# A cast load issued ahead of building the identity, in a sparse 3x3 convolution

## The chip, the cores and the metric

The kernel runs on one core of one Trainium2 chip. The metric is device time in microseconds; the median of the runs counts. The profile is of one execution, and its span runs from the first to the last instruction of the program.

## The reference

The reference is a 3x3 convolution with padding 1 over a batch of 16 images, 64 channels in, 128 channels out, 64x64 pixels, in float32. Nine tenths of the weights are zero, and the reference skips those; the result is that of a dense convolution.

```python
batch, c_in, h, w, c_out, k = 16, 64, 64, 64, 128, 3
...
for kh in range(k):
    for kw in range(k):
        if weight[co, ci, kh, kw] != 0:
            output[b, co] += weight[co, ci, kh, kw] * x_pad[b, ci, kh:kh+h, kw:kw+w]
```

## The kernel before

Images are taken in eight pairs. A pair fills the 128 partitions: 64 channels of one image, 64 of the other. Each pair is worked in four blocks of 16 rows. TensorE multiplies each image's half with the weights of one tap (64 x 128) and adds up the taps in PSUM (`product`, L120 to L141).

There are two kinds of block. A direct block (`direct`, L143) sums all nine taps, 8 rows at a time; ScalarE and VectorE copy the sums to the output tile `o`. Only the first block of the first pair is direct. All the others are of the kind `twos` (L150): GpSimd adds two neighbouring rows to `s` (L153), TensorE multiplies `s` with the middle row of taps once for both, ScalarE copies this shared part to `pc` (L160), TensorE makes the rest for even and for odd rows, and VectorE adds the two parts into `o` (L167). So a direct block doesn't need GpSimd, and all later blocks do. It also needs only the rows at the top of the image.

The order on every engine is the order of the program text (`manual_schedule`): nothing is moved by a scheduler, and each engine works through its own list, waiting where it must.

The opening is laid out as follows. SyncE issues two plain loads: the weights (`w_sb`, L60), and the first 18 rows of pair 0 as float32 (`x_head`, L62). GpSimd builds a 128x128 identity in bf16 (`make_identity`, L64: one MEMSET and one select by index, in masks.py). After it, still on GpSimd, comes the load of the first pair's other 46 rows (L65), which casts float32 to bf16 on its way into `xs[0]`, and then seven cast loads of whole pairs (L67). SyncE's loads go through the hardware queue q1, GpSimd's cast loads through the software queue q0; in each queue the transfers stand in the order of their issue.

Meanwhile TensorE runs 27 multiplications of zeros (L74). When the weights have landed, VectorE and ScalarE cast them to bf16 (L91), TensorE transposes them by multiplying with the identity (L97, the first reader of `ident`), and the results are copied to `wT` (L110 to L114, differences at L101). When `x_head` has landed, VectorE casts its first nine rows and ScalarE the other nine (L87), into the upper rows of `xs[0]`. The direct block (TensorE, L134) reads these. The first `s` reads rows 16 to 31, so it needs the load of L65.

A pair's two output tiles are stored by SyncE, 2 MB each (L187); for the last pair in halves of 1 MB (L184). Seven output tiles take turns. At the end SyncE waits for the stores (L213, launch code).

Of the kernel before, what the change touches and what calls it, by code (L numbers as in the profile page):

```python
# [27 lines left out]
def kernel(  # L28
# [6 lines left out]
    nc = tc.nc  # L35

    B, C_IN, H, W = x.shape
# [3 lines left out]
    HEAD = 18  # L41
# [13 lines left out]
    def pair(p):  # L55
        return x[2 * p : 2 * p + 2].rearrange("n i h w -> (n i) h w")

    xs = [x_pool.tile([128, H, W], BF16, name=f"x{p}") for p in range(NP)]
    w_sb = const_pool.tile([C_OUT, C_IN * KH * KW], FP32, name="w_sb")
    nc.sync.dma_start(out=w_sb, in_=weight.rearrange("o i kh kw -> o (i kh kw)"))  # L60
    x_head = const_pool.tile([128, HEAD, W], FP32, name="x_head")
    nc.sync.dma_start(out=x_head, in_=pair(0)[:, 0:HEAD, :])  # L62
    ident = const_pool.tile([128, 128], BF16, name="ident")
    make_identity(nc, ident)  # L64
    nc.gpsimd.dma_start(out=xs[0][:, HEAD:H, :], in_=pair(0)[:, HEAD:H, :])  # L65
    for p in range(1, NP):
        nc.gpsimd.dma_start(out=xs[p], in_=pair(p))  # L67

# [149 lines left out]
```

## Time and profile before

| what | value |
|---|---|
| median of 6 runs | 127.69 us |
| lowest and highest run | 127.37 and 128.45 us |
| the profiled execution's own time | 127.9 us |
| its span | 126.1 us |
| mean granted TensorE clock | 0.957 |
| busy: PE, DVE, ACT, POOL | 110.5, 82.3, 38.1, 40.7 us |
| DMA packets, bytes, mean rate | 4044, 42.70 MB, 339 GB/s |
| HBM read and written | 17.07 and 33.55 MB |

PE is TensorE, PEld its weight loads, DVE is VectorE, ACT is ScalarE, POOL is GpSimd, SP is SyncE. Starts are microseconds from the span's beginning. The DMA row of the page gives, for each fortieth of the span, the mean busy share of the core's 16 DMA engines, in tenths. A cast load counts with the bytes that it writes, which are half of those it reads. A DMA's time to landing runs from the start of the issuing instruction to the last update of its semaphore. In the waits, a row names who waited, for whom, the total in microseconds, how often, and the longest.

### The profile page before, as it was taken

How to read it: one execution, taken by the hardware profiler on the slowest of the kernel's cores; microseconds unless marked ns; L12 is line 12 of the kernel's file. 1: busy time of each engine (PE TensorE's matmuls, PEld its weight loads, DVE VectorE, ACT ScalarE, POOL GpSimd, SP SyncE). 2: the span in 40 equal slices, each digit the busy share in tenths (PEclk: the TensorE clock that was granted, in tenths of full speed). 3: DMA queues.
4: the chain of work that ended last, by engine and by line, in shares of the span. 5: the costliest groups of instructions: out<-in, count | busy, mean ns of one | idle time of the engine just before them, and what ended most of it. 6: DMA issues, size and time to landing. Idle time of an engine off the chain costs nothing.

```text
span 126.1 us, 2486 instructions
## 1 busy us (share of the span) xinstructions
PE 110.5 (88%) x1002; PEld 56.0 (44%) x1002; DVE 82.3 (65%) x135; ACT 38.1 (30%) x70; POOL 40.7 (32%) x45
## 2 busy tenths in 40 slices
PE   6689999999999999999999999999999999980000
PEld 6433454545454545444554555455545554430000
DVE  0352277777777777777787778777877787773000
ACT  4521533333333333332433333333333333330000
POOL 7807443333333333333333333333333330000000
PEclk9999999999999999999999999999999999997555
DMA  4999999999999999999999999999999999999990
GB/s 128 222 217 208 216 221 223 213 166 333 333 294 340 338 312 317 307 333 307 431 447 416 421 416 436 447 431 408 421 431 452 416 426 426 421 418 418 421 385 29
DMA packets 4044, 42.70 MB, mean 339 GB/s; under 512 B 448, under 2 KB 448, under 8 KB 832
## 3 DMA queue, kind: packets, MB, share of 16 engines
q1 hardware_dynamic: 2880, 34.44, 65.5%
q0 software_dynamic: 1152, 8.09, 31.6%
q8 instruction: 8, 0.13, 0.4%
q14 instruction: 4, 0.03, 0.1%
HBM read 17.07 MB, written 33.55 MB: 401 GB/s over the span
## 4 chain that ended last, share of the span: by engine, by line
PE 83%; DMA 4%; DVE 1%; issue 1%; DVEq 0%; SPq 0%
PE ps L134 83%; DMA x_head<-in_x_dram 4%; DVE o L167 1%; DVEq L213 0%; DVE x L87 0%; SPq L60 0%; DVEq L167 0%
## 5 line engine op out<-in xcount | busy, mean ns | idle before, releaser
L134 PE MATMUL ps<-x,wT 64*128 64x504 bf16 (+3 forms) x780 | 91.5, 382 | 1.5 <-DVE x L87 1.5
L167 DVE TENSOR_TENSOR o<-ps,pc 128x512 f32<-128x512 f32 x124 | 77.8, 686 | 22.1 <-PE ps L134 19.8
L134 PEld LDWEIGHTS <-wT 64*128 64x128 bf16 x966 | 52.5, 96 | 55.0 <-issue 4.9
L153 POOL TENSOR_TENSOR s<-x 128x512 bf16<-128x512 bf16 x31 | 35.6, 1152 | 60.8 <-PE ps L134 42.9
L160 ACT COPY pc<-ps 128x512 f32<-128x512 f32 x62 | 33.3, 589 | 64.0 <-issue 61.8
L134 PE MATMUL ps<-s,wT 64*128 64x512 bf16 (+1 forms) x186 | 25.5, 377 | 0.0
L148 DVE COPY o<-ps 128x512 f32<-128x512 f32 x2 | 1.4, 692 | 4.9 <-PE ps L134 4.9
L74 PE MATMUL ps<-idle_rhs 128*128 128x128 bf16 x27 | 3.1, 313 | 1.0 <-DVE idle_rhs L71 1.0
L67 POOL DMA_DIRECT2D x<-in_x_dram x7 | 3.7, 567 | 0.0
L74 PEld LDWEIGHTS <-idle_rhs 128*128 128x128 bf16 x27 | 2.8, 148 | 1.0 <-DVE idle_rhs L71 1.0
L147 ACT COPY o<-ps 128x512 f32<-128x512 f32 x2 | 1.2, 586 | 6.2 <-PE ps L134 6.2
L91 DVE CAST w_bf<-w_sb 128x192 bf16<-128x192 f32 (+1 forms) x4 | 1.2, 383 | 2.7 <-DMA w_sb<-in_weight_dram 2.7
L91 ACT ACT_TABLE_LOAD x1 | 1.3, 1283 | 0.7 <-PEq L202 0.7
L87 DVE CAST x<-x_head 128x576 bf16<-128x576 f32 x1 | 0.5, 460 | 1.6 <-DMA x_head<-in_x_dram 1.6
L97 PE MATMUL ps<-ident,w_bf 128*128 128x128 bf16 x9 | 1.2, 304 | 0.2 <-DVE w_bf L91 0.2
L91 ACT CAST w_bf<-w_sb 128x64 bf16<-128x64 f32 (+1 forms) x2 | 0.7, 416 | 1.6 <-DMA w_sb<-in_weight_dram 1.6
L97 PEld LDWEIGHTS <-w_bf 128*128 128x128 bf16 x9 | 0.7, 122 | 0.7 <-DVE w_bf L91 0.6
L101 DVE TENSOR_TENSOR wT<-ps,wT 128x384 bf16<-128x384 f32 x2 | 1.0, 548 | 0.0
L87 ACT CAST x<-x_head 128x576 bf16<-128x576 f32 x1 | 0.7, 672 | 0.4 <-DMA x_head<-in_x_dram 0.4
L65 POOL DMA_DIRECT2D x<-in_x_dram x1 | 0.7, 702 | 0.1
L71 DVE MEMSET idle_rhs<- 128x64 uint32 x1 | 0.1, 112 | 0.8 <-PEq L202 0.8
L110 ACT CAST wT<-ps 128x384 bf16<-128x384 f32 x1 | 0.5, 478 | 0.4 <-PE ps L97 0.4
(8 smaller groups left out, 1.9 us busy)
## 6 DMA issues: line engine op xcount, KB each, us to landing
out_dram<-o SPq DMA_DIRECT2D x14, 2048.0 KB, 18.1
x<-in_x_dram POOLq DMA_DIRECT2D x7, 1024.0 KB, 29.6
out_dram<-o SPq DMA_DIRECT2D x4, 1024.0 KB, 10.4
x<-in_x_dram POOLq DMA_DIRECT2D x1, 736.0 KB, 8.6
x_head<-in_x_dram SPq DMA_DIRECT2D x1, 576.0 KB, 5.2
w_sb<-in_weight_dram SPq DMA_DIRECT2D x1, 288.0 KB, 2.9
```

Source lines behind the costliest of these rows:

```text
L67: nc.gpsimd.dma_start(out=xs[p], in_=pair(p))
L74: nc.tensor.matmul(idle_ps, idle_rhs, idle_rhs, start=True, stop=True)
L87: copy(out=xs[0][:, a:b, :], in_=x_head[:, a:b, :])
L91: copy(out=w_bf4[:, g, a:b, :], in_=w_v[:, k : k + b - a, :])
L97: nc.tensor.matmul(wps[:, j, :], src, ident, start=True, stop=True)
L101: nc.vector.tensor_tensor(out=wT[:, g], in0=wps, in1=wT[:, G1], op=SUB)
L134: nc.tensor.matmul(ps[n][:, lo:hi, c_lo:c_hi], tap(g, kw, n), src[q, a:b:step, c_lo + kw - 1 : c_hi + kw - 1], start=(i == 0), stop=(i == ...
L147: nc.scalar.copy(out=o[0][:, r0 : r0 + rows, :], in_=ps[0])
L148: nc.vector.tensor_copy(out=o[1][:, r0 : r0 + rows, :], in_=ps[1])
L153: nc.gpsimd.tensor_tensor(out=s, in0=xs[p][:, r0 : r0 + 16 : 2, :], in1=xs[p][:, r0 + 1 : r0 + 16 : 2, :], op=ADD)
L160: nc.scalar.copy(out=c, in_=shared[n])
L167: nc.vector.tensor_tensor(out=o[n][:, first : r0 + 16 : 2, :], in0=ps[n], in1=pc[n], op=ADD)
```

## The change

The GpSimd load of rows 18 to 63 of pair 0 is issued ahead of the identity's two instructions instead of after them. Everything else, and the order on every other engine, stays as it was.

```diff
@@ -60,9 +60,9 @@
     nc.sync.dma_start(out=w_sb, in_=weight.rearrange("o i kh kw -> o (i kh kw)"))
     x_head = const_pool.tile([128, HEAD, W], FP32, name="x_head")
     nc.sync.dma_start(out=x_head, in_=pair(0)[:, 0:HEAD, :])
+    nc.gpsimd.dma_start(out=xs[0][:, HEAD:H, :], in_=pair(0)[:, HEAD:H, :])
     ident = const_pool.tile([128, 128], BF16, name="ident")
     make_identity(nc, ident)
-    nc.gpsimd.dma_start(out=xs[0][:, HEAD:H, :], in_=pair(0)[:, HEAD:H, :])
     for p in range(1, NP):
         nc.gpsimd.dma_start(out=xs[p], in_=pair(p))
```

## The prediction

> **What bounds the kernel now.** I read the page from its end: first the DMA part, then the chain, then the waits of SyncE's queue, then GpSimd's own timeline, and last the DMA view cut into short stretches of the opening. The span in 40 slices, and the queues, come first:
>
> ```profile
> span 126.1 us, 2486 instructions
> ...
> PE   6689999999999999999999999999999999980000
> ...
> DMA  4999999999999999999999999999999999999990
> ...
> q1 hardware_dynamic: 2880, 34.44, 65.5%
> q0 software_dynamic: 1152, 8.09, 31.6%
> ```
>
> PE is full from the third slice on, but it stops 12 us before the end, while the DMA row is full from the second slice to the last but one. The queues' packets took 65.5 + 31.6 + 0.4 + 0.1 = 97.6% of what 16 engines have, 123.1 us of 126.1. The first packet starts at 1.77 us, so some 123 us of transfers lie between 1.77 us and the end. The chain "that ended last" follows compute instructions, and ends with VectorE:
>
> ```profile
> 113.87 0.60 DVE o L167
> ```
>
> That is 114.47 us; 11.6 us of span come after it. SyncE's waits say what for:
>
> ```profile
> SPq L187 <- DVE o L167: 94.9, 14, 22.6
> SPq L184 <- DVE o L167: 10.5, 4, 5.3
> SPq L213 <- DMA out_dram<-o: 9.2, 4, 2.4
> ```
>
> The last row is the closing wait for the stores. The issues and their times to landing show the backlog behind it:
>
> ```profile
> out_dram<-o SPq DMA_DIRECT2D x14, 2048.0 KB, 18.1
> x<-in_x_dram POOLq DMA_DIRECT2D x7, 1024.0 KB, 29.6
> out_dram<-o SPq DMA_DIRECT2D x4, 1024.0 KB, 10.4
> x<-in_x_dram POOLq DMA_DIRECT2D x1, 736.0 KB, 8.6
> x_head<-in_x_dram SPq DMA_DIRECT2D x1, 576.0 KB, 5.2
> ```
>
> A 2 MB store alone is 2.097 MB / 0.425 TB/s (the mean of 62 to 114 us) = 4.9 us, but its median is 18.1 us, and the shortest of all 18 stores took 8.6 us. Each store found at least 8.6 - 4.9 - 1.0 (issue to first packet, as for w_sb: 0.74 to 1.77) = 2.7 us of other transfers ahead of it. So I take the kernel to be bound by its DMA engines, with PE 3 to 4 us ahead of them. The chain's 83% PE names the longest compute chain, not the end.
>
> The opening, as GpSimd lived it (start, length, instruction):
>
> ```profile
> 0.73 0.20 POOL masks.py:197 MEMSET ident<- 128x128 bf16 x1 [0.29 <-POOLq L202]
> 1.01 0.29 POOL masks.py:199 TENSOR_SCALAR_AFFINE_SELECT ident<-ident 128x128 bf16<-128x128 bf16 x1
> 1.43 0.70 POOL L65 DMA_DIRECT2D x<-in_x_dram  x1
> 2.12 3.71 POOL L67 DMA_DIRECT2D x<-in_x_dram  x7
> 10.20 3.35 POOL L153 TENSOR_TENSOR s<-x 128x512 bf16<-128x512 bf16 x3 [4.37 <-DMA x<-in_x_dram]
> ```
>
> The load that moves is issued at 1.43 and lands 8.6 us later, about 10.0. GpSimd then waits for it and makes s at 10.20; PE takes up s only at 13.64 us, after the direct block. And the DMA view of 3.60 to 4.38 us, whole, has one queue alone in it:
>
> ```profile
> DMA packets 38, 0.17 MB, mean 219 GB/s; under 512 B 1, under 2 KB 1, under 8 KB 38
> ## 3 DMA queue, kind: packets, MB, share of 16 engines
> q1 hardware_dynamic: 38, 0.17, 95.7%
> ```
>
> No packet of GpSimd's queue (q0) moves before 4.39 us, 2.96 us after its issue. Engines had gone straight from weights to x_head (the first x_head packets start at 2.70, the last engine's at 3.28), and in the packet records an engine that finishes x_head goes on to q0 some 6 ns later, never before. Only the first to finish stood idle, from 4.27 to 4.39.
>
> **What the Trainium skill says.** "DMA: Bandwidth & Descriptors", section "Issuing engines are not separate DMA queues": transfers issued by SyncE and GpSimd run on the same 16 engines, and a second issuer saves issue time only. The trace agrees: every engine is taken from 1.77 us on, by q1 and then q0. Its section "Queues, rings and completion order" says an engine alternates between queues at packet boundaries, a packet being several descriptors. Here no x_head piece was split by q0, as if all that one engine carries of x_head were one such packet; that fits, though one trace can't prove it. Its section "Latency and other measured facts" gives about 1 us to the first byte on GpSimd's path; this trace has 2.96 us from issue, or 2.26 us from the end of the 0.70 us instruction, and I use those.
>
> **The change part by part.** Nothing is added or removed: the same ten GpSimd instructions, in another order.
>
> The load of rows 18 to 63 moves past the MEMSET (0.20), the select (0.29) and the gaps between them: 1.43 - 0.73 = 0.70 us earlier, so issued at 0.73. It moves past no DMA on its own queue; on SyncE's side it is now issued beside w_sb (0.74) and before x_head (1.16), where it used to come after both. With the same 2.96 us its first packet could start at 3.69 instead of 4.39. All engines have begun x_head by 3.28, so it still queues behind x_head on each. Direct gain: the one idle spell, 4.39 - 4.27 = 0.12 us of one engine in 16, or 0.01 us of DMA time.
>
> The identity moves 0.70 us later: MEMSET at 1.43, select done at about 1.30 + 0.70 = 2.00. Its reader, the first transpose (L97), starts at 4.22 after w_bf, cast from weights that land at 3.64. It is hidden by 2.2 us of waiting for weights; without that cover it would cost 0.70 us of PE's start, which itself has 3 to 4 us of stores to hide behind.
>
> The seven loads at L67 start where they did, 2.12, as the sum of the work ahead of them is unchanged: 0.
>
> If the load does land up to 0.7 us sooner, the first s is made sooner; PE wants it at 13.64, and it was there at 11.35: 0.
>
> What is not visible in the trace of before is how the engines behave when q0 becomes ready earlier. There is a slow stretch: 354 GB/s at 2.8 to 3.6 us, 219 at 3.60 to 4.38, though only x_head moves. From 4.38 to 6.2, x_head's 0.15 MB and q0's 0.18 MB written (0.36 read, for q0 casts 4 bytes to 2) are 0.51 MB in 1.82 us, 280 GB/s, against about 2 x 210 = 420 at 10 to 15 us. Lost: 0.78 x (1 - 219/420) + 1.82 x (1 - 280/420) = 0.37 + 0.61 = about 1.0 us. Its cause I can't read: it starts while GpSimd issues (until 5.83) and before q0 moves. Upper end of a gain: all of it goes, -1.0. Upper end of a loss: it starts 0.7 us earlier and ends when it did, 0.7 x 0.48 = +0.3, or it covers everything from 2.0 us, 1.6 x 0.48 = +0.8. I take 0, as the seven issues that fill 2.12 to 5.83 stay put.
>
> The sum: 126.1 - 0.01 + 0 + 0 = 126.1 of span, with 1.8 us around it 127.9 as profiled. The median of the runs, 127.69, is 0.2 below that execution; on it the likeliest is 127.6 to 127.7. Half a per cent, 0.64 us, is about what this kernel's measurement tells from no change; the six runs alone spread over 1.1 us.
>
> **Rivals.** *Gain (chance 0.22).* An earlier ready q0 lets engines flow from x_head into it without the slow stretch. In its favour: in the packet records the two engines that reached q0 first, at 4.39 and 4.47, needed 2.3 and 2.1 us for a first piece that takes 0.46 later, as if it weren't quite ready. Against: the end is set by the slowest engine, and the slowest at the end (124.51 us; the next was done near 123.7) shows its delay after 62 us, not here. Worth -0.7 to -1.0, from 127.69: 126.9.
>
> *Slower (0.16).* The slow stretch is what an engine does with both queues alive, and now begins 0.7 us or more earlier, during weights and x_head. The stretch began 0.8 us before q0's first packet. It decides if that packet comes at 3.0 us or sooner, 2.3 us after the new issue or less: then weights and x_head run at about 219 GB/s from 2.2 us on, 1.4 x 0.48 = +0.7, up to the +0.8 above: 128.5. x_head itself would land later than 6.38 and PE start later than 6.92, but that costs nothing until PE's 3 to 4 us are used up.
>
> *The compute chain decides (0.03, inside the last).* If q0 got ahead of x_head's packet on an engine, x_head would wait for 8 x 0.455 = 3.6 us there, and PE start at 10.5; with the last stores then needing 4.9 + 1.5 us after PE's end, about 124.9 to 125.5 against 125.0 now: no more than +0.5.
>
> *It doesn't do what it says.* In the built program the load does stand ahead of MEMSET and select, so this is no rival for the order; it is one for the time, since the transfer is hidden anyway. That is my forecast.
>
> **How the numbers follow.** No change 0.62, at 127.6, own range 127.1 to 128.2; gain 0.22 at 126.9; slower 0.16 at 128.5. The range takes in the gain's middle and most of the loss: 126.9 to 128.5. A few of the gain case's outcomes stay inside half a per cent, and a few of the first case's drift out with the spread of runs; the chances stay 0.22, 0.62, 0.16.
>
> **What would show it.** Right: L65 starts near 0.73 and the select ends near 2.0; L67 from 2.1; transposes still from about 4.2; the first q0 packet near 3.7 to 4.3, with x_head landing within 0.3 us of 6.38; the DMA row full from the second slice on; the last compute near 114.5 and the span within 0.6 us of 126.1. Wrong: x_head landing near or after 7 us, with a low GB/s from 2 us on (the slower rival), or over 350 GB/s, reads counted, right through 3.6 to 5.8 us and a span near 125.3 (the gain). The forecast also fails if the DMA row shows holes after 62 us, since then PE's start would count after all.

## The result, and the profile after

The changed kernel took 127.56 us in the median of 35 runs, and the kernel before 127.79 in 72 runs beside it: ratio 0.9979, 95% interval 0.9964 to 0.9994. The medians are over all runs; the ratio leaves out those in a slower state, four of the 35. By the ratio it is 0.27 us less: a gain clear of the noise, but less than half of the half per cent below which the prediction spoke of no change. The forecast was 127.6. The lowest runs are nearly alike (127.23 and 127.31): what the change did is bring more runs near them. 28 of the 72 runs before lay under 127.65 us, and 22 of the 35 after.

The profiled execution has these lines in the page's head and slices:

```profile
span 125.6 us, 2486 instructions
...
PE   6588999999999999999999999999999999910000
...
DMA  4999999999999999999999999999999999999980
```

The picture is that of before: DMA engines taken from the second slice to the end, PE done some 15 us ahead of it (13 before). The chain of work ends with

```profile
111.17 0.60 DVE o L167
```

which is 2.7 us sooner than before, while the span is only 0.5 us shorter. In SyncE's waits that time comes back as a longer closing wait for the stores (9.2 before, 12.1 now):

```profile
SPq L187 <- DVE o L167: 91.9, 14, 19.9
SPq L213 <- DMA out_dram<-o: 12.1, 4, 4.9
```

and in the issues, with KB and median time to landing, into longer queues for the stores (18.1 and 10.4 before):

```profile
out_dram<-o SPq DMA_DIRECT2D x14, 2048.0 KB, 20.1
x<-in_x_dram POOLq DMA_DIRECT2D x7, 1024.0 KB, 31.3
out_dram<-o SPq DMA_DIRECT2D x4, 1024.0 KB, 12.5
x<-in_x_dram POOLq DMA_DIRECT2D x1, 736.0 KB, 8.4
x_head<-in_x_dram SPq DMA_DIRECT2D x1, 576.0 KB, 4.9
```

GpSimd's opening, by its timeline:

```profile
1.23 0.70 POOL L63 DMA_DIRECT2D x<-in_x_dram  x1 [0.79 <-POOLq L202]
1.92 0.23 POOL masks.py:197 MEMSET ident<- 128x128 bf16 x1
2.22 0.29 POOL masks.py:199 TENSOR_SCALAR_AFFINE_SELECT ident<-ident 128x128 bf16<-128x128 bf16 x1
2.46 3.73 POOL L67 DMA_DIRECT2D x<-in_x_dram  x7
9.75 3.36 POOL L153 TENSOR_TENSOR s<-x 128x512 bf16<-128x512 bf16 x3 [3.55 <-DMA x<-in_x_dram]
```

The load starts at 1.23, only 0.20 us sooner than before, and not at 0.73, where the MEMSET used to start. As GpSimd's first instruction here, the DMA issue began 0.50 us later than the MEMSET had; in the kernel before, MEMSET and select filled that time. The other loads start 0.34 us later than before. The moved load's first packet starts at 4.54 us, 3.31 us after the issue, and so later than before (4.39, 2.96 us after). Yet it lands at 1.23 + 8.4 = 9.6 instead of 10.0, and x_head at 6.1 instead of 6.4. The stretch of 3.60 to 4.38 us has the same queue alone, at the same pace:

```profile
DMA packets 38, 0.18 MB, mean 224 GB/s; under 512 B 0, under 2 KB 0, under 8 KB 38
```

The difference comes after it. In the DMA view of 4 to 7 us, the kernel before:

```profile
DMA packets 127, 0.59 MB, mean 197 GB/s; under 512 B 16, under 2 KB 16, under 8 KB 127
## 3 DMA queue, kind: packets, MB, share of 16 engines
q0 software_dynamic: 61, 0.36, 67.2%
q1 hardware_dynamic: 66, 0.23, 37.1%
```

and the changed one:

```profile
DMA packets 142, 0.68 MB, mean 226 GB/s; under 512 B 16, under 2 KB 16, under 8 KB 142
## 3 DMA queue, kind: packets, MB, share of 16 engines
q0 software_dynamic: 76, 0.45, 74.6%
q1 hardware_dynamic: 66, 0.23, 30.0%
```

As many packets of x_head, but 15 more of the moved load. That is one place where the two executions differ; the experiments ask whether the gain comes from there, and whether TensorE, 2.7 us sooner, has a part in it.

### The profile page after: what moved, and what is told of

It is laid out like the page before. It is cut to its first block, busy times and chain, and to the rows that moved or that the text cites. A ratio compares the mean times of both kernels' runs of the same rounds, so it can differ in the third digit from the quotient of the medians.

```text
span 125.6 us, 2486 instructions
## 1 busy us (share of the span) xinstructions
PE 107.4 (86%) x1002; PEld 58.5 (47%) x1002; DVE 82.3 (66%) x135; ACT 38.1 (30%) x70; POOL 40.7 (32%) x45
## 4 chain that ended last, share of the span: by engine, by line
PE 78%; DMA 7%; issue 1%; DVE 1%; POOL 1%; DVEq 0%; POOLq 0%
PE ps L134 78%; DMA x<-in_x_dram 7%; DVE o L167 1%; POOL s L153 1%; DVEq L213 0%; POOLq L153 0%; POOLq L202 0%; DVEq L167 0%; POOLq masks.py:199 0%
## 5 line engine op out<-in xcount | busy, mean ns | idle before, releaser
L134 PE MATMUL ps<-x,wT 64*128 64x504 bf16 (+3 forms) x780 | 88.8, 373 | 1.5 <-DVE x L87 1.5
L134 PEld LDWEIGHTS <-wT 64*128 64x128 bf16 x966 | 55.1, 94 | 49.9 <-issue 1.9
```

Of the source, the lines that this page charges most:

```text
L134: nc.tensor.matmul(ps[n][:, lo:hi, c_lo:c_hi], tap(g, kw, n), src[q, a:b:step, c_lo + kw - 1 : c_hi + kw - 1], start=(i == 0), stop=(i == ...
```

## The experiments

Every kernel was timed beside the kernel before, and the ratios are to that. Three theories stood: **opening** (the engines move more in the first 8 us, and the end follows), **gap** (the half microsecond that the identity now puts between the first cast load and the others is what helps), and **pace** (TensorE's direct block took 6.9 us in the profile before and 4.0 in that after; runs with the slow pace are the long ones, and the change only makes them rarer).

**The two kernels once more**, unchanged.

> The changed kernel once more, as it is, beside the others on the same chip. If the small gain is there: ratio 0.9965 to 0.9995. A second profile tells what repeats: x_head landing near 6.1 and the moved load near 9.6 (they were 6.4 and 10.0 before), its issue near 1.23, the later loads from 2.46; and whether TensorE's direct block takes 4.0 us again as in the first profile after, or 6.9 as before. If the direct block's pace is a matter of chance, it differs without the end differing.

> The kernel before once more, as it is, for a second profile of the opening. If the first profile was typical: x_head lands near 6.4, the moved load near 10.0, and the span is 0.4 us longer than the changed kernel's. If the first was one of the long runs by chance (its 127.9 us are above the median): x_head near 6.1, the load near 9.7, span near 125.7. Ratio 1.000 within 0.0015.

Measured: 0.9979 (0.9963 to 0.9995) for the changed kernel, 0.9989 (0.9970 to 1.0008) for that of before. So the gain repeats. The second profiles are less plain. In that of the changed kernel x_head landed at 6.6 and the moved load at 10.1, later than expected (6.1 and 9.6). In that of before they landed at 6.4 and 10.4, as a typical one should, but its span was not 0.4 us longer than the changed kernel's: it was 125.5 us against 125.6. A span of one execution doesn't show the gain, then; why, comes out below. And the second profile of before has TensorE's direct block at the fast pace, with no change made:

```profile
6.95 3.98 PE L134 MATMUL ps<-x,wT 64*128 64x512 bf16 x36 [1.50 <-DVE x L87]
```

The pace is a matter of chance in the kernel before, so TensorE's 2.7 us between the first two profiles need not be the change's doing. In the traces' clock records the full clock is first recorded at 12.9 us in the first profile of before, at 5.3 in the second and at 4.6 in the first of the changed kernel, which fits the three paces. "TensorE: Matmul & The Clock Gate" of the Trainium skill, section "Part 1: The HAM clock gate", describes a free-running window of activity that decides when the matrix clock comes up; chance of this kind fits that (4.0 to 6.9 us were seen for this block), though no run here shows the window.

**Is it TensorE's pace?** Two kernels: that of before with 60 instead of 27 multiplications of zeros (the full clock is recorded from 6.5 us on, ahead of the block), and the changed one with 4.

```diff
-    for _ in range(27):
+    for _ in range(60):
```

and

```diff
-    for _ in range(27):
+    for _ in range(4):
```

> The kernel before, with nothing but 60 instead of 27 multiplications of zeros, so that TensorE's clock is up before the direct block whenever x_head lands. Theory 'pace of the direct block': the long runs of the kernel before are those in which the direct block runs slowly (6.9 us instead of 4.0), so that the stores come 2 us later and the engines run short of them late in the run; the change makes such runs rarer, and does nothing else. Then this kernel has no long runs either: ratio to before 0.996 to 0.998, at or under the changed kernel's 0.9979, lowest runs as before, few above 127.65 us. Theory 'opening': the gain comes from the transfers of the first 10 us alone; then the multiplications change nothing: 0.999 to 1.001, long runs as often as before.

> The changed kernel with 4 instead of 27 multiplications of zeros, so that TensorE has done little when the direct block starts and that block should run slowly (6 to 7 us) in every run. Theory 'pace of the direct block': the gain is gone, ratio to before 1.000 to 1.004, most runs above 127.65 us. Theory 'opening': ratio 0.997 to 0.999 like the changed kernel.

Measured: before with 60 0.9994 (0.9977 to 1.0011), its block at 3.98 us; changed with 4 0.9983 (0.9966 to 1.0000), its block at 6.53 us. Timed side by side, the two have medians of 127.71 and 127.43 us, and 9 and 16 of 22 runs under 127.65. The theory of pace had the opposite order. The gain stays with the load's place, and the theory of pace falls, though the two ratios' intervals overlap.

**Is it the gap?** The kernel before with two MEMSETs between the load and its followers; and the changed kernel with the identity behind all loads, so without the gap.

```diff
     nc.gpsimd.dma_start(out=xs[0][:, HEAD:H, :], in_=pair(0)[:, HEAD:H, :])
+    pad = const_pool.tile([128, 128], BF16, name="pad")
+    for _ in range(2):
+        nc.gpsimd.memset(pad, 0.0)
     for p in range(1, NP):
```

and

```diff
     nc.gpsimd.dma_start(out=xs[0][:, HEAD:H, :], in_=pair(0)[:, HEAD:H, :])
-    ident = const_pool.tile([128, 128], BF16, name="ident")
-    make_identity(nc, ident)
     for p in range(1, NP):
         nc.gpsimd.dma_start(out=xs[p], in_=pair(p))
+    ident = const_pool.tile([128, 128], BF16, name="ident")
+    make_identity(nc, ident)
```

> The kernel before with two MEMSETs of 128x128 on GpSimd between the first cast load (L65, where it was, at 1.43) and the seven later loads, which so start at about 2.65 instead of 2.12. The change did two things to the queue: it issued the first load 0.20 us earlier and opened a gap of 0.5 us after it. If the gap alone brings the gain: ratio 0.997 to 0.999. If the earlier issue brings it: 0.999 to 1.001.

> The changed kernel with the identity built after all eight cast loads, so that the first load keeps its new place (1.23) and the later ones follow at once (1.93 instead of 2.46), without a gap. The identity is ready only near 6.2, the transposes move from 4.3 to 6.3 and TensorE's first block to about 8.5. If the earlier issue brings the gain: ratio 0.996 to 0.999, in spite of TensorE's 1.5 to 2 us of delay. If the gap brings it: 0.999 to 1.001. If TensorE's chain decides: 1.008 or more.

Measured: gap alone 1.0000 (0.9984 to 1.0016); identity last 1.0001 (0.9983 to 1.0018). The gap alone brings nothing. The second kernel is not as clean as was hoped: its opening is that of the changed kernel (load landed at 9.3), but the gain is not in its time. TensorE stood idle for 2.4 us before the transposes, waiting for the identity, and its last store was issued at 114.5. But the changed kernel with 4 multiplications had its last store as late (114.6) and kept its gain. By its time alone the identity-last kernel came out as the theory of the gap had it. The times so leave open that the gain needs both, the earlier load and the gap after it; the records below speak against that, for one execution.

**A later queue.** Ten MEMSETs ahead of the first cast load of the kernel before.

```diff
     make_identity(nc, ident)
+    pad = const_pool.tile([128, 128], BF16, name="pad")
+    for _ in range(10):
+        nc.gpsimd.memset(pad, 0.0)
     nc.gpsimd.dma_start(out=xs[0][:, HEAD:H, :], in_=pair(0)[:, HEAD:H, :])
```

> The kernel before, with ten more MEMSETs of a 128x128 tile on GpSimd ahead of the first cast load, so that all of GpSimd's loads are issued about 2.0 us later (L65 near 3.4, first packet of its queue near 6.4). DMA-opening theory (time is set by how fully the 16 engines work in the first 7 us, and the slow stretch of x_head belongs to GpSimd's queue coming alive): x_head runs at 350 to 400 GB/s throughout and lands near 4.8 to 5.2, then engines stand idle until about 6.4, some 1.5 us each; set against the 1.0 us of slow stretch that is gone, the end is 0.3 to 0.8 us later, ratio 1.002 to 1.006. Rival, slow stretch belongs to x_head itself: x_head still lands at 6.1 to 6.4, engines idle 0.5 to 1 us in the mean and the later load adds that: 1.004 to 1.010. Rival, compute chain decides: PE starts when x_head lands, the first s comes 2 us later, near 12.2, still before PE wants it if PE runs at the pace of before: 1.000.

Measured: 1.0084 (1.0055 to 1.0113), the load issued at 3.75 (3.4 was expected), its first packet at 5.15 (6.4 was expected), x_head landed at 5.2. The DMA view of 2.80 to 4.30 us shows x_head without the slow stretch,

```profile
DMA packets 173, 0.62 MB, mean 413 GB/s; under 512 B 22, under 2 KB 22, under 8 KB 173
```

where the changed kernel has

```profile
DMA packets 115, 0.44 MB, mean 293 GB/s; under 512 B 11, under 2 KB 11, under 8 KB 115
```

and then, from 4.3 to 5.2 us, little moved at all:

```profile
DMA packets 27, 0.09 MB, mean 97 GB/s; under 512 B 10, under 2 KB 10, under 8 KB 27
```

So the slow stretch goes with GpSimd's first cast load, and x_head alone doesn't have it. But to be rid of it in this way is dear: the engines waited for the queue, and nearly all then needed 0.7 to 1.6 us for the first piece of the cast load, which takes 0.46 later. The end is 1.1 us later than before, for 2.3 us of delay in the issue. The expected 1.002 to 1.006 was too low, as it did not count those slow first pieces.

**The followers later.** Fifteen MEMSETs between identity and the seven loads of the changed kernel.

```diff
     make_identity(nc, ident)
+    pad = const_pool.tile([128, 128], BF16, name="pad")
+    for _ in range(15):
+        nc.gpsimd.memset(pad, 0.0)
     for p in range(1, NP):
```

> The changed kernel, with fifteen more MEMSETs on GpSimd between the identity and the seven later loads, so that those are issued about 3 us later (from 5.5 instead of 2.46), while the load that was moved keeps its place. If the slow stretch (x_head at about 220 GB/s from 3.6 us) comes from the issuing of the seven loads: x_head lands near 4.9 to 5.2 instead of 6.1, the tail of pair 0 near 8.6, and the end is 0.7 to 1.0 us earlier, ratio to before 0.990 to 0.994. If it comes from the first cast load coming alive, or from x_head itself: x_head lands at 6.1 as in the changed kernel, the later loads are still queued in time (the tail lands at 9.6), ratio 0.997 to 0.999 as for the changed kernel.

Measured: 1.0033 (1.0012 to 1.0054), slower than the changed kernel beside it (0.9979), and outside both of the ranges expected; x_head at 6.0 and the first load at 9.5, as in that one. The slow stretch is not due to the issuing of the seven loads. A part of the loss is at the next joint, where the engines go on from the first cast load to the second. From 8.0 to 10.5 us this kernel has

```profile
DMA packets 81, 0.49 MB, mean 197 GB/s; under 512 B 16, under 2 KB 16, under 8 KB 33
```

against, in the changed kernel with 60 multiplications,

```profile
DMA packets 92, 0.58 MB, mean 231 GB/s; under 512 B 16, under 2 KB 16, under 8 KB 36
```

The followers are issued from 6.58, and engines begin to be through with the first load at 8.3: twelve of the first pieces of pair 1 took 0.7 to 1.3 us instead of 0.62. So slow first pieces were seen at both joints at which engines reached a cast load soon after its issue. They don't account for the whole loss: by 20 us this kernel had read 6.98 MB, and the changed kernels of the table below 7.06 in the mean. At 0.42 MB per us that is an estimated 0.2 us, of 0.7 us lost in time.

**The records of the kernels side by side.** By the traces' records of single packets: of the 128 pieces (packets) of the first cast load, how many took over 0.65 us, and the longest; what the loads and stores had moved by 8.0 and by 62 us (a cast piece counts twice its written bytes); when the load landed; the span of that execution.

| kernel | load issued | long pieces, longest | MB by 8 us | MB by 62 us | landed | span | ratio |
|---|---|---|---|---|---|---|---|
| before | 1.43 | 2, 2.31 us | 1.82 | 24.56 | 10.0 | 126.1 | |
| before again | 1.43 | 6, 2.30 | 1.85 | 24.81 | 10.4 | 125.5 | 0.9989 |
| before, gap | 1.43 | 11, 2.33 | 1.79 | 24.63 | 10.2 | 125.8 | 1.0000 |
| before, 60 | 1.42 | 7, 2.65 | 1.82 | 24.72 | 10.4 | 125.6 | 0.9994 |
| before, late queue | 3.75 | 21, 1.55 | 1.53 | 24.18 | 10.8 | 127.1 | 1.0084 |
| changed | 1.23 | 1, 1.05 | 2.00 | 24.74 | 9.6 | 125.6 | 0.9979 |
| changed again | 1.24 | 0 | 1.91 | 24.77 | 10.1 | 125.6 | 0.9979 |
| changed, 60 | 1.24 | 0 | 1.97 | 24.82 | 9.6 | 125.5 | 0.9970 |
| changed, 4 | 1.24 | 0 | 1.95 | 24.84 | 9.9 | 125.5 | 0.9983 |
| changed, identity last | 1.25 | 2, 1.23 | 2.02 | 24.74 | 9.3 | 126.0 | 1.0001 |

With the load at 1.43 the four profiles have 2 to 11 long pieces, the longest of each over 2.2 us, and 1.82 MB in the mean by 8 us. With the load at 1.23 to 1.25 the five at the foot of the table have 0 to 2, none over 1.3 us, and 1.97 MB. The four other kernels with the load at 1.24 (late followers; 110 and 220 multiplications and x_head issued by ScalarE, both below) have none, and 1.98 to 2.05 MB. The long pieces are enough to make the difference: the time above 0.46 us, summed over the 128 pieces and divided by 16 engines, is 0.43 us in the mean of the four and 0.05 in that of the five. And 0.15 MB at the full 0.42 MB per us is an estimated 0.36 us; the measured gain is 0.27. The lead is still 0.16 MB in the mean at 20 us, and 0.10 at 62.

The spans of single executions don't follow it, because of a second slow stretch, as the first stores begin. The page's GB/s row tells of it in slices 8 and 9 (22 to 28.4 us). Here are those of before, before again, and changed:

```profile
GB/s 128 222 217 208 216 221 223 213 166 333 333 294 340 338 312 317 307 333 307 431 447 416 421 416 436 447 431 408 421 431 452 416 426 426 421 418 418 421 385 29
GB/s 122 233 212 221 217 214 211 217 285 334 345 306 329 319 303 311 337 308 332 402 423 413 418 433 444 439 420 418 418 428 444 439 423 423 423 410 420 428 373 16
GB/s 127 245 220 222 211 214 217 190 300 321 342 300 336 339 297 300 342 308 318 383 430 423 412 438 438 428 430 423 412 438 433 428 433 428 415 417 417 428 368 23
```

Cast loads alone show as some 215, half of what they read, and stores lift the row above 300. In between, the first falls to 166 and the third to 190, and the second doesn't fall. From 20 to 30 us, reads counted in full, the profiles moved between 3.98 and 4.29 MB. That is an estimated 0.7 us from end to end, more than the change is worth, and it doesn't go by the load's place: 4.01 to 4.23 with the load at 1.43, 4.05 to 4.19 in the five below. It does go with the stores. In the kernel with 220 multiplications, whose first store is issued at 31.2 instead of 21.6 to 25.2, these ten microseconds have no such fall (4.29, the most of all), and it comes at about 34. So before again, slow in the opening, lost next to nothing here and ended at 125.5, while changed lost its lead over it here and ended at 125.6. The identity-last kernel had moved as much as changed by 8 us and by 62 us, and still ended 0.4 us after it: its loss lies later, and what made it stays open. In this one execution, then, the opening without the gap was worth as much as with it.

The theory of the opening fits the records and, in the mean, the time. What is shown is that the load's place and the long pieces go together in all profiles, that a much later issue is slower, and that neither the gap alone nor TensorE's pace brings the gain. What isn't shown: that the earlier issue without the gap is enough, since the time of the identity-last kernel didn't bear it out; and whether it is the 0.20 us that matter, or that the load is GpSimd's first instruction, since no run has the one without the other.

**How much of TensorE is hidden?** The changed kernel with 60, 110 and 220 multiplications; of the three, the first edit is

```diff
-    for _ in range(27):
+    for _ in range(60):
```

> The changed kernel with 60 instead of 27 multiplications of zeros ahead of the transposes, so that TensorE reaches the transposes near 7.8 instead of 4.2 (half that delay if its clock comes up), and the direct block near 9 instead of 6.6. DMA theory: TensorE has 3 us or more of stored-up transfers to hide behind, the end does not move: ratio to before 0.996 to 1.000, like the changed kernel beside it. Compute theory: 1.5 to 2.5 us later, ratio 1.010 to 1.020.

> The changed kernel with 110 multiplications of zeros: the direct block starts near 10 instead of 7 us, at full pace, and the last store is issued near 115.2 instead of 112.4. If stores coming later than about 114 us let engines run short (as the profiles with 114.5 and a span of 126.0 to 126.1 suggest): span 126.2 to 126.8, ratio to before 1.002 to 1.007. If 3 us are still hidden: 0.997 to 0.999.

> The changed kernel with 220 instead of 27 multiplications of zeros, so that TensorE comes to the transposes near 16 us and ends near 121 instead of 112. DMA theory: the last pair of 1 MB stores needs about 4.9 us of transfer and 1.5 us around it after VectorE's last sum, so it lands at 127 to 128 instead of 124.5: 2.5 to 4 us later than the changed kernel, ratio to before 1.018 to 1.030, less than half of TensorE's delay. Compute theory (TensorE's delay shows in full): 9 us later, ratio 1.068.

Measured: 0.9970 (0.9954 to 0.9985), 0.9996 (0.9981 to 1.0011), 1.0468 (1.0435 to 1.0501). The second lies between its two expectations. The last store is issued at 112.4, 115.4 and 121.4 us (112.3 in the second profile of the changed kernel), and the spans are 125.5, 125.9 and 131.9 (125.6). So 3.1 us of delay cost 0.3 us of span, and 9.0 us cost 6.3: some 2.7 us are hidden, counted from 112.3, from single executions. The expected 2.5 to 4 us for the last kernel was too low, since it priced only the final stores. In its page the engines run dry twice, in slices 29 and 33:

```profile
DMA  4999999999999999999999999999299919999990
```

Stores of 2 MB come in pairs every 12.8 us and need 9.8 us a pair (twice 4.9); with TensorE this late, the queue empties before two of the pairs, those issued at 95.1 and 107.9 us.

**A version that goes further.** The changed kernel with 60 multiplications, and x_head issued by ScalarE, so beside the weights.

```diff
-    nc.sync.dma_start(out=x_head, in_=pair(0)[:, 0:HEAD, :])
+    nc.scalar.dma_start(out=x_head, in_=pair(0)[:, 0:HEAD, :])
```

> The changed kernel with 60 multiplications of zeros and x_head issued by ScalarE instead of SyncE, so at 0.73 beside the weights and not at 1.17 behind them. If the engines' slow start (about 230 GB/s from 1.6 to 2.8 us) is for want of queued pieces: x_head and the first cast load land 0.2 to 0.4 us sooner, ratio to before 0.993 to 0.996. If both share what there is: the weights land later (4.2 instead of 3.7), x_head no sooner, 0.997 to 0.999.

Measured: 0.9960 (0.9946 to 0.9973), 127.26 us, with 21 of 22 runs under 127.65. It is clearly faster than the kernel before, and has the lowest ratio here; from the changed kernel with 60 multiplications (0.9970) its interval doesn't part it. By the issues' times to landing the second expectation came true, though its ratio (0.997 to 0.999) did not:

```profile
x<-in_x_dram POOLq DMA_DIRECT2D x1, 736.0 KB, 8.3
x_head<-in_x_dram ACTq DMA_DIRECT2D x1, 576.0 KB, 5.3
w_sb<-in_weight_dram SPq DMA_DIRECT2D x1, 288.0 KB, 5.0
```

Weights and x_head shared the engines: the weights landed 2 us later, at 5.8 (4.2 was expected), x_head at 6.0 and the cast load at 9.5, hardly sooner than with SyncE as its issuer (6.0 and 9.6). The transposes didn't need the weights sooner, as the multiplications of zeros held TensorE to 6.8 us. What this kernel gains over the one with 60 multiplications, if anything, no run separates.

## Why the prediction was right, point by point

**The number: near, and in part by luck.** The forecast was no change, at 127.6 from a median of 127.69. The kernel before then measured 127.79, and the change took off 0.2 per cent by a mechanism to which the sum had given 0.01 us. Moreover the change made was smaller than the one reckoned with: the load moved by 0.20 us, not by 0.70.

**What bounds the kernel: right.** 2.7 us gained by TensorE between the two profiles left the span within 0.5 us, and one kernel with TensorE 3.1 us later lost 0.3. The hidden amount was mis-sized: the 3 to 4 us counted from 114.5 measured 2.7 counted from 112.3, so about half a microsecond from 114.5. The estimate looked at the queue ahead of the last stores, and not at the moments between the pairs at which it is shortest.

**The identity at no cost: right.** It was ready at 2.51 (I had 2.00), and the transposes started at 4.23 (4.22 before).

**The load 0.70 us earlier: wrong in size.** It was 0.20, and the followers moved by +0.34 instead of 0: the step "issued at 0.73" took the MEMSET's start for the load's. The 0.50 us that the issue needed as GpSimd's first instruction isn't visible in the trace of before, where other work fills them. And the first packet came no sooner: the prediction added its 2.96 us to the new issue and had it at 3.7 to 4.3, and it started at 4.54.

**The direct gain of 0.01 us: this step failed, though the sum held.** It counted engines standing idle between x_head and the cast load, and found 0.12 us on one. The cost sat in the first pieces themselves: in the profile before, two that took 2.3 and 2.1 us instead of 0.46, which I had seen and put to the rival of the gain. By the records they are what the changed kernel is rid of: 2 to 11 of them, an estimated 0.4 us of all engines' time. The rival's sign, slow first pieces, was the right one; it was wrong in its size (0.7 to 1.0 us) and in that the slow stretch would go: at 3.60 to 4.38 us it is there as before, 224 against 219 GB/s.

**The slow stretch as the loss of 1.0 us: not borne out.** The late-queue kernel did away with it and was slower, though it also made the engines wait, so what the stretch costs stays open. It looks as if the engines, during the stretch, already work at the cast load's first pieces, and what they lose on x_head they save afterwards; no record shows this directly, and it stays an inference. Open, too, is how long before its use a cast load must have been issued: "DMA: Bandwidth & Descriptors", section "Latency and other measured facts", has about 1 us to the first byte on this path; here an idle engine began 1.4 us after the issue (3.75 to 5.15), with up to 1.6 us for its first piece. In the five changed kernels of the table the load's first packet came 3.2 to 3.6 us after the issue, and nearly all pieces were quick; in the four with the load at 1.43 it came 2.8 to 3.0 us after it. But in one of these (before, 60) a piece that began 4.0 us after the issue still took 1.66 us. So the records give no fixed time.

**The rival on the slower side: did not happen.** x_head landed between 6.0 and 6.9 us in the changed kernel's own profiles and in those with other counts of multiplications up to 60, and the DMA row has no hole. With TensorE later still the row does get holes, as the kernel with 220 multiplications shows.

## What to carry to other kernels

Where the DMA engines set the end, as here, ask of an instruction's place in the opening what it does to their work, and not only what it does to the compute chain. In this kernel, cast loads that the engines reached soon after their issue began with slow pieces, at the first joint and, with late followers, at the second; so it is worth trying to have such a load in its queue well before the one ahead of it is through. When the gain is two parts in a thousand, profile each kernel more than once, and look for stretches elsewhere that vary by as much: two profiles of the same kernel differed by 2 us in TensorE's last instruction, and by 0.2 MB in what the engines moved as the first stores began, for no reason in the code.

## What was not expected of the hardware

GpSimd's first DMA issue began 0.50 us later than a MEMSET in the same place (1.23 against 0.73). First pieces of a cast load took up to 2.65 us, where later ones take 0.46. For some two to three microseconds as the first stores joined the cast loads, the engines moved less than at full pace, by up to 0.3 MB and by an amount that varied between executions of one kernel. And with x_head on ScalarE's queue the weights landed at 5.8 instead of 3.7 us, so the two queues shared the engines within a load.
